# A hybrid encoder layer on one core: two engines instead of one for the first RMS norm of the third and fourth blocks of rows

## The chip, the cores and the metric

The kernel runs on one core of a Trainium2 chip. The core has five engines that each work through a queue of their own in order: TensorE (PE, with its weight loads shown as PEld), VectorE (DVE), ScalarE (ACT), GpSimd (POOL) and SyncE (SP), which here issues nearly all DMAs. The metric is the device time of one execution in microseconds (us), lower is better. The kernel before takes 2622.69 us, the median of 3 runs (2622.18 to 2624.44).

## The reference

One layer of a bidirectional encoder, batch 1, 2048 rows of 1024 features, all float32:

```python
h = rms_norm(x, norm_mix)                      # x: 2048 x 1024
z = h @ w_in                                   # 1024 x 4352
q_a, k_a, v_a, q_b, k_b, v_b, g_a, g_b = split(z)
y_a = windowed_gqa(q_a, k_a, v_a, sink)
y_b = neighborhood_attn(q_b, k_b, v_b, rpb)
gates = sigmoid(concat(g_a, g_b) + b_gate)
x = x + (gates_a * (y_a @ w_proj_a) + gates_b * (y_b @ w_proj_b)) @ w_out
x = x + square(relu(rms_norm(x, norm_mlp) @ w_up)) @ w_down
return rms_norm(x, norm_final)
```

with

```python
def rms_norm(x, g):
    var = mean(x * x, axis=-1)
    return x * rsqrt(var + 1e-6) * g
```

What matters here is the very first norm, `rms_norm(x, norm_mix)`, for rows 1024 to 2047.

## The kernel before

**Blocks and precision.** The 2048 rows are four blocks of 512 rows; a block is four tiles of 128 rows x 1024 features. Every matrix product is made of three matmuls (`mm3`, `mm3s`, lines 200 to 202 and 297 to 299) of operands that are split into a high and a low part: high x high, high x low, low x high. ScalarE makes the high part (a cast, line 293), VectorE the low part (a subtraction, line 294).

**The input projection.** Blocks 0 and 1 go through `w_in` together. A 2 x 2 scheme needs seven products instead of eight; their order is `ORDER = (1, 2, 5, 6, 7, 4, 3)` (line 369). The columns of `w_in` come in nine groups, numbered q = 0 to 8 below (`QUADS`); q = 5 to 8 are the gate columns. For each group a generator `in_quad` runs the seven products. A product has two halves (a = 0, 1) of 12 matmuls of 128x512, each half in a PSUM bank of its own. A bank is used by several products in turn, so between two of them a result must be read out: product 6's bank is read by VectorE (`add(V, u2[a], ps, c1[a])`, line 290) before product 7 writes the same bank, and product 7's before product 4. The operands of a group's seven products come from `in_left`: sums on VectorE (line 290) and splits (lines 293 and 294).

**The third and fourth block.** In column group q = 5 the rows of the third block (b = 2), in q = 6 those of the fourth (b = 3), are prepared beside the products: `x_tiles` loads four tiles (SP, line 362, four DMAs a tile; `xin` has three buffers, the fourth tile lies in the buffer of `in_v2`, tile name `zv2`, shown as `zv`). `normalised(..., by_scalar=True)` then scales every row by the reciprocal root of its mean square: per tile two ScalarE squares with an accumulated sum (line 236), one small VectorE sum of both (line 239), one GpSimd power to -0.5 (line 241), one ScalarE multiplication of the 128x1024 tile by it (line 248). After the third, fourth, fifth and sixth product in program order `turned_out` transposes a quarter of the four tiles each (four VectorE transposes of 128x256, line 260, into a buffer `ze`) and stores it with four DMAs (line 268) to `h1d`, from where later stages load it.

**Shared buffers.** The ring `ze` (`in_e`) has two buffers of 128x1024. Three users share it: the unused outputs of the squares (class `Junk`: `in_e()[:, 0]`), the gate columns that ScalarE copies out of PSUM after product 2 (line 468, stored by line 475), and the four quarters of `turned_out`.

**What sets the order.** The kernel gives priorities by program order; a scheduler places each engine's instructions in a fixed order when the kernel is built. Each engine and SP then run in that order and wait on semaphores. Up to product 7 of q = 5 TensorE's order is the same in both kernels, and from product 2 of q = 7 on the order of every engine is the same again.

Of the kernel before, what the change touches and what calls it, by code (L numbers as in the profile page):

```python
# [8 lines left out]
F32 = mybir.dt.float32  # L9
F32R = mybir.dt.float32r  # L10
AF = mybir.ActivationFunctionType
ALU = mybir.AluOpType
# [3 lines left out]
D = 1024  # L16
# [5 lines left out]
EPS = 1e-6  # L22
P = 128
# [69 lines left out]
def encoder_layer(ctx, tc, x, norm_mix, w_in, b_gate, sink, rpb, w_pa, w_pb, w_out,  # L93
                  norm_mlp, w_up, w_down, norm_final, dist_a, mask_b, out):
    nc = tc.nc
    V, A, G, PE, SY = nc.vector, nc.scalar, nc.gpsimd, nc.tensor, nc.sync

    def pool(name, side=None, space=None, stack=None):
        kw = {"reuse_waits": "tile"} if space is not DRAM else {}
        if side:  # L100
            kw["side"] = side
        if space:
            kw["space"] = space
        return (stack or ctx).enter_context(tc.tile_pool(name=name, bufs=1, **kw))

    def pools(stack, side, tags, name):

        return {t: pool(f"{name}_{t}", side=side, stack=stack) for t in tags}

    cp = pool("cp", side="left")  # L110
# [13 lines left out]
    def T(pl, shape, dt, tag, bufs):  # L124
        n_t[0] += 1
        pl = pl[tag] if isinstance(pl, dict) else pl
        return pl.tile(shape, dt, tag=tag, bufs=bufs, name=f"{tag}_{n_t[0]}")
# [7 lines left out]
    power = cr.tile([P, 1], F32, name="power")  # L135
# [77 lines left out]
    def load_tile(pl, tag, bufs, rows):  # L213
        t = T(pl, [P, D], F32, tag, bufs)
        last_dma[0] = SY.dma_start(t, rows).ins
        return t

    def rstd_shared(pl, t):

        st = T(pl, [P, 4], F32, "st", 4)  # L220
        junk = T(pl, [P, 512], F32, "junk", 1)
        A.activation(junk, t[:, 0:512], AF.Square, accum_out=st[:, 0:1])
        other = T(pl, [P, 512], F32, "junkv", 1)
        V.tensor_tensor_reduce(out=other, in0=t[:, 512:1024], in1=t[:, 512:1024], scale=1.0, scalar=0.0,
                               op0=ALU.mult, op1=ALU.add, accum_out=st[:, 1:2])
        r = st[:, 2 : 3]
        V.scalar_tensor_tensor(out=r, in0=st[:, 0:1], scalar=D * EPS, in1=st[:, 1:2], op0=ALU.add, op1=ALU.add)
        G.tensor_tensor(out=r, in0=r, in1=power, op=ALU.pow)
        return r

    def rstd_of(pl, t, jp=None, mean=False):

        st = T(pl, [P, 4], F32, "st", 4)
        junk = T(pl if jp is None else jp, [P, 512], F32, "junk", 1)
        for n in range(2):
            A.activation(junk, t[:, n * 512 : (n + 1) * 512], AF.Square, scale=float(D) ** -0.5 if mean else 1.0,
                         accum_out=st[:, n : n + 1])
        r = st[:, 2 : 3]
        V.scalar_tensor_tensor(out=r, in0=st[:, 0:1], scalar=EPS if mean else D * EPS, in1=st[:, 1:2],
                               op0=ALU.add, op1=ALU.add)  # L240
        G.tensor_tensor(out=r, in0=r, in1=power, op=ALU.pow)
        return r

    def normalised(pl, tiles, jp=None, by_scalar=False):

        for t in tiles:
            if by_scalar:
                A.activation(t, t, AF.Copy, scale=rstd_of(pl, t, jp, True))
            else:
                V.tensor_scalar(t, t, rstd_of(pl, t, jp), float(D) ** 0.5, ALU.mult, ALU.mult)  # L250

    def turned_out(d, ht, tiles, g, gain=None, queue=None):

        hv = ht.rearrange("p (j t c) -> p t j c", j=8, t=4)
        for t in range(4):
            V.transpose(out=hv[:, t], in_=tiles[t][:, g * 256 : (g + 1) * 256].rearrange("p (j c) -> p j c", j=8))  # L260
        h3 = ht.rearrange("p (j x) -> p j x", j=8)
        if gain is not None:
            (step, n), _ = gain.ap
            gv = bass.AP(gain.tensor, gain.offset + 8 * g, [[step, n], [1, 8], [0, P]])
            V.tensor_tensor(out=h3, in0=h3, in1=gv, op=ALU.mult)
        dv = d.rearrange("(j i) (a x) -> a i j x", i=32, a=4)
        for a in range(4):
            (queue or SY).dma_start(dv[a][:, 8 * g : 8 * g + 8], h3[32 * a : 32 * a + 32])
# [49 lines left out]
    s_z = ExitStack()  # L318
# [14 lines left out]
    xp = pools(s_x, "left", ("xin",), "x0")  # L333
# [20 lines left out]
    def x_tiles(pl, b, bufs):  # L354
        out = []
        for t in range(4):
            xt = T(pl, [P, D], F32, "xin", bufs) if t < bufs else in_v2[0]()
            if b > 1:

                for a in range(4):  # L360
                    r = b * BT + a * P + t * 32
                    SY.dma_start(xt[32 * a : 32 * a + 32], xf[r : r + 32])
            else:
                r = b * BT + t * P
                last_dma[0] = SY.dma_start(xt, xf[r : r + P]).ins
            out.append(xt)
        return out
# [3 lines left out]
    def in_weights(c, w):  # L371

        return [row_half(c, w, p) for p in range(2)]
# [8 lines left out]
    def in_left(ws, w, skip=(), behind=None):  # L382

        a11, a21 = ws[0][:, :, 0:w], ws[0][:, :, w : 2 * w]
        a12, a22 = ws[1][:, :, 0:w], ws[1][:, :, w : 2 * w]

        def parts(src, eng):
            return left_parts(src, w, eng)

        s1, s2 = None, None  # L390
        for n in ORDER:
            if n in skip:
                continue
            with tc.issue_after(behind[0]) if behind else nullcontext():
                if n == 5:
                    s1 = in_sum()[:, :, 0:w]
                    add(V, s1, a21, a22)
                elif n == 6:
                    add(V, a21, a11, a21, ALU.subtract)
                    s2 = in_sum()[:, :, 0:w]  # L400
                    add(V, s2, a22, a21, ALU.subtract)
                elif n == 3:
                    add(V, a12, a12, s2, ALU.subtract)
            yield parts({1: a11, 2: a12, 5: s1, 6: s2, 7: a21, 4: a22, 3: a12}[n], V)
# [137 lines left out]
    for t in tiles[0]:  # L542
        V.tensor_scalar(t, t, rstd_shared(xp, t), float(D) ** 0.5, ALU.mult, ALU.mult)
    right = {n: (in_page[n](), in_page[n]()) for n in (1, 2)}
# [15 lines left out]
    for n, t in enumerate(tiles[1]):  # L560
        V.tensor_scalar(t, t, rstd_shared(xp, t), float(D) ** 0.5, ALU.mult, ALU.mult)
# [10 lines left out]
    for p in range(2):  # L572
        t = T(xp, [P, D], F32, "xin", 8).rearrange("p (k c) -> p k c", k=4)
# [54 lines left out]
    def bias_tables():  # L628
        rp = rpb[0]
        for n, (w, lo_rel) in enumerate(((24, -8), (32, -8), (24, -15))):  # L630
            tb = in_e()[0:BH].rearrange("h a b -> h (a b)")[:, 0 : T_ROWS * w]
            tb3 = tb.rearrange("h (r w) -> h r w", w=w)
            G.memset(tb, 0.0)
            ncol = min(w, 15 - lo_rel + 1)
            first = 15 + lo_rel
            SY.dma_start(tb3[:, T_RO - 7 : T_RO + 8, 0:ncol], rp[:, :, first : first + ncol])

            G.tensor_scalar(tb, tb, 8.0, 1.0, ALU.mult, ALU.mult)
            SY.dma_start(tabs[n], tb)

    for q in range(2, len(QUADS)):
        if q == 5:
            s_v.close()
            in_v2.pop()
            xp = pools(s_z, "right", ("xin", "st"), "x2")
        if q == 7:
            bias_tables()
        lf = list(in_left(ws, 256, (1, 2) if q == 2 else ()))
        if q + 1 < len(QUADS):
            ws = in_weights(*QUADS[q + 1])  # L650
        if q in (5, 6):

            b = q - 3
            xt = x_tiles(xp, b, 3)
            normalised(xp, xt, Junk(), by_scalar=True)
        ops2.extend(lf if q == 2 else ())
        for n, _ in enumerate(quad2 if q == 2 else in_quad(*QUADS[q], iter(lf), right)):
            if q in (5, 6) and 2 <= n < 6:
                turned_out(h1d[b - 2], in_e().rearrange("p k x -> p (k x)"), xt, n - 2)
# [677 lines left out]
    for b in range(NB):  # L1337
# [43 lines left out]
        for t in range(4):  # L1381
            row0 = b * BT + t * P
            xt = load_tile(p4x, "xr", 5, xf[row0 : row0 + P])
# [25 lines left out]
    for m in range(2):  # L1409
        right = next(rights)  # L1410
# [225 lines left out]
```

## Time and profile before

| | value |
|---|---|
| median of 3 runs | 2622.69 us (2622.18 to 2624.44) |
| the profiled execution | 2621.88 us |
| its span | 2620.1 us, so 1.8 us lie around it |
| TensorE busy | 99% of the span |
| VectorE busy | 62% |
| ScalarE busy | 47% |
| GpSimd busy | 14% |
| TensorE idle, 210 to 250 us (third block) | 0.0 us |
| TensorE idle, 250 to 290 us (fourth block) | 3.15 us |

In rows of a timeline the first column is the start in us from the beginning of the span, the second the time (of one instruction, or of several merged ones), then the engine, the line, the operation, the tiles written and read, the shape and the count; in square brackets stands how long the engine was idle before, and what released it. In rows of a table by stretches the columns are, for each engine, busy us and number of instructions, then the granted TensorE clock, the DMA share and GB/s. Line numbers are those of the kernel before.

### The profile page before, as it was taken

The numbers are of one execution on the slowest core, as the hardware profiler recorded it, in microseconds if no ns is written. First come the engines' busy times: TensorE is split into PE (matmuls) and PEld (weight loads), VectorE is DVE, ScalarE is ACT, GpSimd is POOL, SyncE is SP. The second block draws the span as 40 slices with busy tenths as digits, with TensorE's granted clock in tenths as the row PEclk, the third lists the DMA queues.
The fourth block names the chain that finished last, engine by engine and source line by source line (L and its number), as shares of the span: only waits on it lengthen the run. The fifth ranks groups of instructions, "written<-read, shape, count | busy, mean of one in ns | idle before, by whom it ended". The sixth has DMA issues, their size and how long they took to land.

```text
span 2620.1 us, 34509 instructions
## 1 busy us (share of the span) xinstructions
PE 2586.9 (99%) x12140; PEld 2149.8 (82%) x12140; DVE 1625.1 (62%) x2653; ACT 1239.8 (47%) x2261; POOL 358.1 (14%) x431
## 2 busy tenths in 40 slices
PE   8999999999999999999999999999999999999999
PEld 6888788778888888888888888888888888888887
DVE  8765666665544444755567777776656534555766
ACT  5335256666555555633334554644544322322454
POOL 1000114344555541000001000100000000000010
PEclk9999999999999999999999999999999999999999
DMA  5657485455876655954556655854428825445555
GB/s 184 200 156 200 141 243 159 114 155 145 240 219 180 191 144 164 318 177 151 179 178 208 245 205 202 302 191 149 153 101 300 300 101 182 146 146 171 183 194 170
DMA packets 353982, 490.30 MB, mean 187 GB/s; under 512 B 28792, under 2 KB 188664, under 8 KB 351632
## 3 DMA queue, kind: packets, MB, share of 16 engines
q1 hardware_dynamic: 346752, 471.04, 56.8%
q10 hardware_dynamic: 7056, 17.04, 1.8%
q8 instruction: 96, 1.57, 0.2%
q14 instruction: 78, 0.64, 0.1%
HBM read 328.54 MB, written 159.45 MB: 186 GB/s over the span
## 4 chain that ended last, share of the span: by engine, by line
PE 88%; DVE 4%; DMA 4%; ACT 2%; issue 1%; SPq 1%; POOL 0%; DVEq 0%; POOLq 0%; ACTq 0%
PE b L297 15%; PE b L299 15%; PE b L298 15%; PE mm L200 6%; PE mm L202 6%; PE mm L201 6%; PE zb L297 3%; PE zb L299 3%; PE zb L298 2%; PE pt L200 2%; PE pt L201 2%; PE pt L202 2%; PE av L967 2%; PE pt L955 2%; PE s L927 2%
## 5 line engine op out<-in xcount | busy, mean ns | idle before, releaser
L298 PE MATMUL b<-dwh,dah 128*128 128x512 f32 x896 | 348.5, 389 | 0.0
L299 PE MATMUL b<-dwh,dah 128*128 128x512 f32 x896 | 347.6, 389 | 0.0
L297 PE MATMUL b<-dwh,dah 128*128 128x512 f32 x896 | 339.6, 389 | 0.0
L293 ACT CAST dah<-da 128x1024 fp32r<-128x1024 f32 (+1 forms) x128 | 120.9, 945 | 368.6 <-PE b L299 241.8
L294 DVE TENSOR_TENSOR dah<-da,dah 128x1024 fp32r<-128x1024 f32 (+1 forms) x128 | 139.7, 1091 | 224.1 <-ACT dah L293 221.1
L297 PE MATMUL b<-ubh,uwhlb 128*128 128x512 f32 x592 | 230.3, 389 | 0.0
L298 PE MATMUL b<-ubh,uwhlb 128*128 128x512 f32 x592 | 230.3, 389 | 0.0
L299 PE MATMUL b<-ubh,uwhlb 128*128 128x512 f32 x592 | 229.3, 389 | 0.1
L200 PE MATMUL mm<-hT,whl 128*128 128x512 f32 x544 | 218.2, 401 | 0.0
L202 PE MATMUL mm<-hT,whl 128*128 128x512 f32 x544 | 215.1, 395 | 0.0
L201 PE MATMUL mm<-hT,whl 128*128 128x512 f32 x544 | 213.7, 393 | 0.0
L298 PEld LDWEIGHTS b<-dwh,dah 128*128 128x128 f32 x896 | 168.2, 188 | 35.0
L299 PEld LDWEIGHTS b<-dwh,dah 128*128 128x128 f32 x896 | 168.2, 188 | 34.9
L297 PEld LDWEIGHTS b<-dwh,dah 128*128 128x128 f32 x896 | 168.2, 188 | 34.9
L297 PE MATMUL zb<-zh,zwhl 128*128 128x512 f32 x476 | 186.7, 394 | 7.9 <-DVE zc L290 3.4
L298 PE MATMUL zb<-zh,zwhl 128*128 128x512 f32 x476 | 186.4, 392 | 0.0
L299 PE MATMUL zb<-zh,zwhl 128*128 128x512 f32 x476 | 183.7, 392 | 0.3 <-DVE zwhl L294 0.3
L290 DVE TENSOR_TENSOR uc<-b,uc 128x512 f32<-128x512 f32 x160 | 109.2, 689 | 104.2 <-PE b L299 103.2
L1506 POOL TENSOR_TENSOR st<-st,power 128x1 f32<-128x1 f32 x16 | 13.3, 841 | 925.0 <-DVE st L1505 924.9
L297 PEld LDWEIGHTS b<-ubh,uwhlb 128*128 128x128 f32 x592 | 111.1, 188 | 23.8 <-issue 0.4
L299 PEld LDWEIGHTS b<-ubh,uwhlb 128*128 128x128 f32 x592 | 111.1, 188 | 23.5 <-DVE uwhlb L294 0.5
L298 PEld LDWEIGHTS b<-ubh,uwhlb 128*128 128x128 f32 x592 | 111.1, 188 | 23.1
(253 smaller groups left out, 5912.5 us busy)
## 6 DMA issues: line engine op xcount, KB each, us to landing
at<-uc SPq DMA_DIRECT2D x224, 256.0 KB, 2.0
da<-at SPq DMA_DIRECT2D x96, 512.0 KB, 3.7
dw<-in_w_down_dram SPq DMA_DIRECT2D x160, 256.0 KB, 4.8
uraw<-in_w_up_dram SPq DMA_DIRECT2D x32, 1024.0 KB, 6.8
raw<-in_w_in_dram SPq DMA_DIRECT2D x34, 512.0 KB, 4.7
zraw<-in_w_in_dram SPq DMA_DIRECT2D x16, 1024.0 KB, 7.7
z<-zg SPq DMA_DIRECT2D x64, 256.0 KB, 5.1
qa<-qs_a SPq DMA_DIRECT2D x32, 256.0 KB, 8.3
```

Of the source, the lines that this page charges most:

```text
L200: PE.matmul(ps, lh, rh, start=first, stop=False)
L201: PE.matmul(ps, lh, rl, start=False, stop=False)
L202: PE.matmul(ps, ll, rh, start=False, stop=last)
L290: return eng.tensor_tensor(out=out, in0=a, in1=b, op=op).ins
L293: A.copy(hi, src)
L294: return eng.tensor_tensor(out=lo, in0=src, in1=hi.bitcast(F32), op=ALU.subtract).ins
L297: PE.matmul(ps, lh, rh, start=first, stop=False, skip_group_check=True)
L298: PE.matmul(ps, lh, rl, start=False, stop=False, skip_group_check=True)
L299: PE.matmul(ps, ll, rh, start=False, stop=last, skip_group_check=True)
L927: PE.matmul(ps[:, :n], q[:, i, :], kv[:, z, B_R0[i] // 4 : (B_R0[i] + B_NR[i]) // 4, 4 * B_C0[j] : 4 * (B_C0[j] + w)], start=z == 0, stop= ...
L955: PE.transpose(pt[:kp, at + (i - i0) * P : at + (i - i0 + 1) * P], s[i][:, rr : rr + kp], ident)
L967: last = PE.matmul(po[:, i0 * P : (i0 + ni) * P], v[:kp, c, :], src[:kp, o : o + ni * P], start=first, stop=(c == 7 and z == 1), skip_grou ...
```

## The change

For the third and fourth block the tiles 0 and 2 keep their two ScalarE squares. Tiles 1 and 3 get both squares from VectorE: two `tensor_tensor_reduce` of 128x512 with an accumulated sum, whose unused output goes to a tile of its own, `junkv` (one buffer of 128x512), not into the ring `ze`. All four tiles are multiplied by their factor on VectorE (`tensor_scalar`, 128x1024) and none on ScalarE. The constants move with it (the sum instead of the mean of the squares, then a factor 32). The small tiles `st` come from the pool of constants, and `xin` has a pool of three buffers as before.

```diff
+    def rstd_by_vector(pl, t):
+
+        st = T(pl, [P, 4], F32, "st", 4)
+        other = T(pl, [P, 512], F32, "junkv", 1)
+        for n in range(2):
+            half = t[:, n * 512 : (n + 1) * 512]
+            V.tensor_tensor_reduce(out=other, in0=half, in1=half, scale=1.0, scalar=0.0,
+                                   op0=ALU.mult, op1=ALU.add, accum_out=st[:, n : n + 1])
+        r = st[:, 2 : 3]
+        V.scalar_tensor_tensor(out=r, in0=st[:, 0:1], scalar=D * EPS, in1=st[:, 1:2], op0=ALU.add, op1=ALU.add)
+        G.tensor_tensor(out=r, in0=r, in1=power, op=ALU.pow)
+        return r
...
         if q == 5:
             s_v.close()
             in_v2.pop()
-            xp = pools(s_z, "right", ("xin", "st"), "x2")
+            xp = pools(s_z, "right", ("xin", "junkv"), "x2")
+            xp["st"] = cp
...
             b = q - 3
             xt = x_tiles(xp, b, 3)
-            normalised(xp, xt, Junk(), by_scalar=True)
+
+            for n, t in enumerate(xt):
+                r = rstd_by_vector(xp, t) if n % 2 else rstd_of(xp, t, Junk())
+                V.tensor_scalar(t, t, r, float(D) ** 0.5, ALU.mult, ALU.mult)
```

## The prediction

> **What bounds the kernel now.** I read the page first, then the busy time by stretches, then TensorE's waits where the change sits, then each engine's timeline there.
>
> ```profile
> span 2620.1 us, 34509 instructions
> PE 2586.9 (99%) x12140; PEld 2149.8 (82%) x12140; DVE 1625.1 (62%) x2653; ACT 1239.8 (47%) x2261; POOL 358.1 (14%) x431
> ```
> ```profile
> 210.00:250.00 40.00, 40.00 (x180) 33.16 (x179) 25.90 (x42) 18.18 (x32) 2.19 (x4) 1.00 0.80 231
> 250.00:290.00 40.00, 36.85 (x161) 29.61 (x160) 24.73 (x42) 18.48 (x32) 8.38 (x9) 1.00 0.67 197
> ```
> ```profile
> 264.05 0.39 PE L298 MATMUL zb<-zh,zwhl 128*128 128x512 f32 x1
> 264.27 0.39 PE L299 MATMUL zb<-zh,zwhl 128*128 128x512 f32 x1
> 267.58 0.47 PE L297 MATMUL zb<-zh,zwhl 128*128 128x512 f32 x1 [2.92 <-DVE zc L290]
> ...
> 273.38 0.39 PE L297 MATMUL zb<-zh,zwhl 128*128 128x512 f32 x1
> ```
>
> TensorE is busy 99% of the span, so the time is its work plus its idle time. A matmul follows the last one after 0.227 us (264.05 to 264.27). In the third block's stretch (210 to 250) it never idles; in the fourth's (250 to 290) it idles 3.15 us. Of these, 2.92 are one wait at 264.66: product 7 of q = 6 may not write its bank before VectorE has read product 6 out (zc, L290). So at most 3.15 us can be gained here, and whatever delays a VectorE read-out past TensorE's arrival is lost one for one. The last row is product 4's start.
>
> Why was that read-out late? VectorE and ScalarE before it:
>
> ```profile
> 261.37 0.57 ACT L468 COPY ze<-zb 128x512 f32<-128x512 f32 x1
> ...
> 264.30 0.77 DVE L260 STREAM_TRANSPOSE ze<-xin 128x256 f32<-128x256 f32 x2 [2.57 <-DMA zg<-ze]
> 264.99 1.18 DVE L294 TENSOR_TENSOR zwhl<-zraw,zwhl 128x1024 fp32r<-128x1024 f32 x1
> ...
> 266.78 0.65 DVE L290 TENSOR_TENSOR zc<-zb,zc 128x512 f32<-128x512 f32 x1
> ```
>
> ScalarE was behind with squares and scalings, so its gate copy into ze came late, its store freed the buffer late, VectorE idled 2.57 us and then had four transposes and a split ahead of the read-out. The edit aims at this chain.
>
> **The third block, step by step.** Prices:
>
> ```profile
> 3.99 0.69 DVE L224 CUSTOM_DVE_ANT_0 junkv<-xin 128x512 f32<-128x512 f32 x1 [3.99 <-DMA xin<-in_x_dram]
> 4.60 0.08 DVE L224 DVE_READ_ACCUMULATOR2_ANT st<- 128x1 f32 x1
> ...
> 6.08 0.75 DVE L543 TENSOR_SCALAR xin<-xin,st 128x1024 f32<-128x1024 f32 x1
> 6.74 0.15 DVE L227 SCALAR_TENSOR_TENSOR st<-st 128x1 f32<-128x1 f32 x1
> ```
> ```profile
> 219.87 0.63 ACT L236 ACTIVATE ze<-xin 128x512 f32<-128x512 f32 x1
> 220.41 0.19 ACT L236 ACTIVATION_READ_ACCUMULATOR ze<-xin 128x1 f32 x1
> ...
> 223.42 1.14 ACT L248 ACTIVATE xin<-xin,st 128x1024 f32<-128x1024 f32 x1
> ```
>
> Counted from start to start, a VectorE square with its read costs 0.69 (0.61 + 0.08), a factor 0.67 (6.08 to 6.74). A block gives VectorE four squares and four factors, 4 x 0.69 + 4 x 0.67 = 5.4 us. It takes from ScalarE four squares (0.54 to the read, 0.62 with it by the estimate that the read adds 0.08 as on VectorE) and four scalings of 1.14: 7.0 us. ScalarE had room for that, VectorE is what TensorE waits for.
>
> ```profile
> 222.92 1.23 DVE L294 TENSOR_TENSOR zwhl<-zraw,zwhl 128x1024 fp32r<-128x1024 f32 x1 [2.14 <-ACT zwhl L293]
> 224.06 0.15 DVE L239 SCALAR_TENSOR_TENSOR st<-st 128x1 f32<-128x1 f32 x1
> 224.13 0.69 DVE L290 TENSOR_TENSOR zc<-zb,zc 128x512 f32<-128x512 f32 x1
> 226.10 0.69 DVE L290 TENSOR_TENSOR zc<-zb,zc 128x512 f32<-128x512 f32 x1 [1.28 <-PE zb L299]
> ```
> ```profile
> 221.23 0.63 ACT L236 ACTIVATE ze<-xin 128x512 f32<-128x512 f32 x1 [0.64 <-DMA xin<-in_x_dram]
> ```
>
> A split costs 1.14, a sum 0.08, a read-out 0.60 (0.69 until it is done). Product 6's first read-out ended at 224.82; TensorE came to product 7 at 226.05 (its second half ended then: 226.10). Slack 1.2. The changed order puts ahead of this read-out: both squares of tile 1 (which lands at 221.2), a sum, the split, tile 0's factor, a sum, tile 3's first square. That is 221.23 + 0.69 + 0.08 + 0.69 + 1.14 + 0.67 + 0.08 + 0.69 = 225.3, read out by 226.0. The slack is gone; I take 0.2 us of stall (0 to 0.9).
>
> Product 4 needs product 7's read-out (a second kind of zc). Between the two read-outs now stand, from 225.9: sum 0.08, factor 0.67, square 0.69, factor 0.67, product 6's second read-out 0.60, four transposes 4 x 0.34, sum 0.08, split 1.14, two transposes 0.68, and itself 0.69: 6.7 us, done at 232.6. TensorE arrives at 226.05 + 0.2 + 24 x 0.227 = 231.7, so 1.1 us of stall (0.6 to 1.6).
>
> **The fourth block.** A factor waits for GpSimd's power, which now lies on VectorE's path:
>
> ```profile
> 220.93 0.55 POOL L241 TENSOR_TENSOR st<-st,power 128x1 f32<-128x1 f32 x1 [192.49 <-DVE st L239]
> ...
> 255.31 2.00 POOL L241 TENSOR_TENSOR st<-st,power 128x1 f32<-128x1 f32 x2 [26.37 <-DVE st L239]
> ```
> ```profile
> 256.82 1.15 ACT L248 ACTIVATE xin<-xin,st 128x1024 f32<-128x1024 f32 x1 [0.49 <-POOL st L241]
> ```
>
> It takes 0.55 us beside an idle VectorE; the pair of 255.31, beside a 128x1024 VectorE sum, let its first reader go at 256.82, 1.5 us on. So each factor waits 0 to 0.5 us at its place.
>
> The rows of the fourth block load into buffers that the third block's last transposes free:
>
> ```profile
> 239.93 1.10 DVE L260 STREAM_TRANSPOSE ze<-xin 128x256 f32<-128x256 f32 x3 [1.99 <-DMA h1d<-ze]
> ...
> 242.46 0.40 DVE L260 STREAM_TRANSPOSE ze<-zv 128x256 f32<-128x256 f32 x1
> ```
> ```profile
> 233.76 4.92 SPq L268 DMA_DIRECT2D h1d<-ze  x8
> ...
> 253.04 1.76 SPq L362 DMA_DIRECT2D zv<-in_x_dram  x4
> ```
>
> Tile 3's factor now comes after product 7's read-out of the third block, so the first two quarters finish near 236 instead of 235 and their eight stores begin at 235.9, not 233.76. The third quarter waits for a store to land (239.93 before, 242 now), then a read-out (0.60) and a split (1.14) stand ahead of the fourth: transposes end near 246.5 instead of 242.86. SP has four stores and two gate stores ahead of the loads (4 x 0.6 + 0.9) where it had three stores, so the last load leaves near 256.7 instead of 254.8 and tile 1 is there near 256.6.
>
> From there VectorE's order up to product 6's read-out has four squares 2.76, one operand sum 1.14, four small sums 0.32, four factors 2.68, two splits 2.28, eight transposes 2.72, the read-out 0.69: 12.6 us, done at 269.2, with power waits up to 270.5. ScalarE is no longer late there, and the 2.57 us wait for ze goes, but its room is filled by this list. Product 7 starts at 270.0 (269.3 to 270.7) instead of 267.58: +2.4, the third block's stalls contained. Its own stall is then 270.0 - 265.8 = 4.2 us (264.5 + 0.2 + 1.1 = 265.8).
>
> Then product 4:
>
> ```profile
> 271.52 0.68 DVE L290 TENSOR_TENSOR zc<-zb,zc 128x512 f32<-128x512 f32 x1
> 273.60 1.10 DVE L260 STREAM_TRANSPOSE ze<-xin 128x256 f32<-128x256 f32 x3 [1.40 <-DMA h1d<-ze]
> ```
>
> Before, the read-out of product 7 (271.52) stood ahead of the transposes that wait for a store. Now it stands behind them: behind the third quarter (1.36), a split (1.14) and three of the fourth (1.02). The third quarter needs the first one's stores: four issues of 0.6 from 267.9, the last landing 3.8 us after its issue,
>
> ```profile
> h1d<-ze SPq DMA_DIRECT2D x32, 128.0 KB, 3.8
> ```
>
> that is 273.5. So 273.5 + 1.36 + 1.14 + 1.02 + 0.69 + 0.14 (the 267.43 to 267.58 from read-out to matmul) = 277.9 for product 4, where TensorE arrives at 270.0 + 24 x 0.227 = 275.4: a new stall of 2.5 us (0 to 3.3). Against 273.38 before, +4.5 us (2.5 to 6).
>
> **The clock.** An idle TensorE can lose clock:
>
> ```profile
> 52.60 0.47 PE L297 MATMUL zb<-zh,zwhl 128*128 128x512 f32 x1 [1.58 <-DVE zh L521]
> 53.64 0.50 PE L299 MATMUL zb<-zh,zwhl 128*128 128x512 f32 x1 [0.34 <-DVE zwhl L294]
> ...
> 54.87 0.63 PE L297 MATMUL zb<-zh,zwhl 128*128 128x512 f32 x1
> 55.30 0.63 PE L298 MATMUL zb<-zh,zwhl 128*128 128x512 f32 x1
> ```
> ```profile
> 264.30:268.00 3.70, 0.78 (x4) 0.41 (x3) 3.70 (x8) 3.04 (x4) 0.00 (x0) 1.00 0.38 96
> ```
> ```profile
> 55.00:60.00 5.00, 5.00 (x18) 3.96 (x17) 5.00 (x7) 0.00 (x0) 0.00 (x0) 0.72 0.49 117
> ```
>
> After 1.9 us of idling at 51 to 53.6 matmuls came 0.43 us apart (54.87 to 55.30); at a mean clock of 0.72 over 5 us, 1.4 us were lost. After the 2.92 us at 264.66 nothing was: the granted clock stayed 1.00. Two stalls of 4.2 and 2.5 us will likely cost it once; behind the first it lies under the second, behind the second it is paid: 0 to 1.6, I take 0.8. The Trainium skill (TensorE: Matmul & The Clock Gate, "Part 1: The HAM clock gate") says the clock halves after at least one idle window of about 3.4 us, in windows that run freely. By it the 2.5 us stall could cost nothing and the term would be 0, the sum 4.5; the row at 52.60 disagrees, with less than 2 us of idling.
>
> **Sum.** 4.5 + 0.8 = 5.3 us on the profiled 2621.88 gives 2627.2; the median lies 0.8 above that execution, so the forecast is 2628.0 us. From the rest of the kernel I take nothing: every engine's order there is the same.
>
> **The rivals.** 0.2% (about what a measurement of this kernel can tell from no change) is 5.2 us, 2617.4 to 2627.9.
> - *A smaller loss.* If the quarters' stores are issued as early as before, the second stall goes, and 4.5 + 0.8 becomes 1.5 to 3.5: 2624 to 2626. For it: VectorE had idle time there (2.14 and 1.28 us in the rows of 222.92 and 226.10); against it: the fixed order with a read-out behind seven transposes.
> - *A gain.* The edit works: ScalarE's 14 us of work vanish, ze is free early, the read-out of product 6 comes before 264.5. All 3.15 us of idling go: 2619.5. It decides if VectorE's list is done before TensorE arrives, 4.7 us earlier than I add it up.
> - *A larger loss.* Every power beside VectorE takes 1.5 us and the clock halves twice: 1.3 us more at product 7 and 1.6 us of clock: 2630 to 2632. For it the row at 255.31. The Trainium skill (GPSIMD Engine Reference, "8. Key points") says GpSimd contends with VectorE instructions of two SBUF inputs, and the squares are such.
> - *Nothing:* the lost slack is just not used up, 2622.7.
>
> **How the numbers follow.** The forecast (2626 to 2630) 0.40, a smaller loss 0.22, a larger loss 0.24, a gain 0.09, nothing 0.05. The forecast's interval is cut by the 0.2% line; I count 0.26 of its 0.40 as slower, since the clock and the powers push one way. Slower 0.26 + 0.24 = 0.50; faster by over 5.2 us needs more than the stretch's idling, 0.05 for what I don't see; the rest, 0.45, is the same. Leaving out the gain and the far end of the larger loss, the range is 2622.0 to 2632.0; the forecast's own is 2626 to 2630.
>
> **What would show it.** In the changed profile: product 7's wait of q = 6 longer than 2.92 us and still released by VectorE's zc; a second wait of 1 to 3 us at product 4; small waits near 226 and 232; ScalarE's copies near 259 to 261; the fourth quarter's transposes of the third block ending near 246; a clock below 1.00 after 270. I'm wrong if VectorE's zc of product 6 ends before 267, if no second wait comes, or if the difference lies after 300 us.

## The result, and the profile after

| | median us | range | against the kernel before, same chips |
|---|---|---|---|
| before | 2622.42 | 2620.53 to 2628.03 (21 runs) | |
| after | 2626.47 | 2623.75 to 2630.28 (21 runs) | ratio 1.0016, 95% interval 1.0010 to 1.0022 |

The change costs 4.05 us, about 0.15%: less than 0.2%, but the interval of the ratio excludes 1. The forecast of 2628.0 lies 1.5 us above the median.

The profiled execution of the changed kernel took 2623.75 us, the fastest of its 21 runs; 1.8 us lie around its span. First the head of its page, then TensorE's share by stretches (window; its length, then busy us and instructions of PE, PEld, DVE, ACT, POOL; granted clock; DMA share; GB/s):

```profile
span 2621.9 us, 34496 instructions
PE 2586.6 (99%) x12140; PEld 2151.1 (82%) x12140; DVE 1633.6 (62%) x2677; ACT 1227.3 (47%) x2237; POOL 358.9 (14%) x431
```
```profile
210.00:250.00 40.00, 39.03 (x173) 31.80 (x172) 30.00 (x55) 12.21 (x20) 3.45 (x4) 1.00 0.78 224
...
260.00:270.00 10.00, 5.29 (x22) 4.08 (x21) 8.92 (x20) 2.23 (x3) 1.40 (x1) 0.93 0.53 171
270.00:280.00 10.00, 10.00 (x41) 8.12 (x40) 8.08 (x15) 1.06 (x1) 0.00 (x0) 0.90 0.79 220
```

The change did what it says: ScalarE's busy time fell by 12.5 us, VectorE's grew by 8.5. TensorE now idles 0.97 us in the third block's stretch and 4.71 in the fourth's. From the second wait on the granted clock is below 1.00, over 20 us by 0.07 x 10 + 0.10 x 10 = 1.7 us. TensorE's timeline shows both waits:

```profile
231.29 0.47 PE L310 MATMUL zb<-zh,zwhl 128*128 128x512 f32 x1 [0.97 <-DVE zc L303]
...
268.91 0.76 PE L310 MATMUL zb<-zh,zwhl 128*128 128x512 f32 x1 [4.71 <-DVE zc L303]
269.47 0.63 PE L311 MATMUL zb<-zh,zwhl 128*128 128x512 f32 x1
269.90 0.63 PE L312 MATMUL zb<-zh,zwhl 128*128 128x512 f32 x1
...
275.93 0.39 PE L310 MATMUL zb<-zh,zwhl 128*128 128x512 f32 x1
```

231.29 is product 4 of q = 5, 268.91 product 7 of q = 6, 275.93 its product 4. (Line numbers of the changed kernel are 13 higher here: L310 is the old L297, L303 the old L290, L273 the old L260.) From 269.47 on matmuls come 0.43 us apart instead of 0.227. At product 4 of q = 6 no wait is shown. VectorE ahead of these read-outs:

```profile
261.93 1.09 DVE L273 STREAM_TRANSPOSE ze<-xin 128x256 f32<-128x256 f32 x3
...
264.64 0.75 DVE L672 TENSOR_SCALAR zv<-zv,st 128x1024 f32<-128x1024 f32 x1 [0.44 <-POOL st L241]
265.31 1.22 DVE L307 TENSOR_TENSOR zwhl<-zraw,zwhl 128x1024 fp32r<-128x1024 f32 x1
266.44 0.44 DVE L273 STREAM_TRANSPOSE ze<-zv 128x256 f32<-128x256 f32 x1
266.81 1.05 DVE L273 STREAM_TRANSPOSE ze<-xin 128x256 f32<-128x256 f32 x3
267.79 0.40 DVE L273 STREAM_TRANSPOSE ze<-zv 128x256 f32<-128x256 f32 x1
268.11 1.25 DVE L303 TENSOR_TENSOR zc<-zb,zc 128x512 f32<-128x512 f32 x2
271.36 1.10 DVE L273 STREAM_TRANSPOSE ze<-xin 128x256 f32<-128x256 f32 x3 [2.00 <-DMA h1d<-ze]
...
274.82 0.65 DVE L303 TENSOR_TENSOR zc<-zb,zc 128x512 f32<-128x512 f32 x1
```

Product 6's read-out (268.11) stands behind both first quarters' eight transposes and two splits; VectorE is 89% busy from 260 to 270.

**Two yardsticks.** Two executions of one kernel differ by several us elsewhere, so the stretch is measured by itself: from ScalarE's first copy of product 1 of q = 5 to the first matmul of the stage after (first of L200). Before and after:

```profile
206.10 0.59 ACT L498 COPY zc<-zb 128x512 f32<-128x512 f32 x1 [1.47 <-PE zb L299]
```
```profile
361.80 0.40 PE L200 MATMUL mm<-hT,whl 128*128 128x512 f32 x1
```
```profile
204.79 0.59 ACT L511 COPY zc<-zb 128x512 f32<-128x512 f32 x1 [1.47 <-PE zb L312]
```
```profile
365.16 0.40 PE L200 MATMUL mm<-hT,whl 128*128 128x512 f32 x1
```

That is 155.7 us before, 160.4 after: +4.7. (206.10 is the first of product 1's two copies, though the expectation of `e5_layout` below calls it the second.) The second yardstick is when product 6's first read-out of q = 6 starts, from the same copy: 266.78 - 206.10 = 60.7 before, 268.11 - 204.79 = 63.3 after. Times of two profiles are compared from this copy on, never as they stand, since the changed profile reaches it 1.31 us earlier. Both yardsticks are in the table for every run below, with the clock that was lost (in us, worked out as above from the windows of 10 us between 250 and 290).

| run | median minus before, us (ratio, 95% interval) | wait at product 4, q = 5 | wait at product 7, q = 6 | read-out after the copy | clock | stretch |
|---|---|---|---|---|---|---|
| before | | 0 | 2.92 | 60.7 | 0 | 155.7 |
| e5_layout (old work) | -0.6 (0.9991 to 1.0009) | 0 | 3.01 | 61.0 | 1.7 | 158.1 |
| after | +4.05 (1.0010 to 1.0022) | 0.97 | 4.71 | 63.3 | 1.7 | 160.4 |
| e6_after_again | +3.1 (1.0003 to 1.0021) | 0.67 | 5.57 | 63.8 | 3.5 | 162.1 |
| e1_third | +0.7 (0.9994 to 1.0011) | 0.68 | 2.98 | 61.4 | 0 | 157.0 |
| e2_fourth | 0.0 (0.9992 to 1.0010) | 0 | 2.04 | 63.0 | 3.4 | 160.0 |
| e3_squares | +2.8 (1.0003 to 1.0021) | 1.21 | 3.88 | 62.6 | 3.4 | 161.2 |
| e4_factors | +0.9 (0.9993 to 1.0011) | 1.58 | 1.96 | 62.2 | 1.7 | 159.7 |
| e7_before_shift | -3.5 (0.9980 to 0.9998) | 0 | 1.27 | 59.7 | 0 | 154.6 |
| e8_after_shift | -0.4 (0.9991 to 1.0009) | 0.64 | 2.65 | 61.0 | 0 | 156.1 |
| e9_warm | +5.4 (1.0010 to 1.0028) | 0.68 | 1.89 | 63.9 | 0 | 161.0 |
| e10_all_squares | +2.8 (1.0001 to 1.0018) | 0.56 | 3.78 | 62.5 | 1.7 | 159.4 |
| e11_one_tile | -1.7 (0.9982 to 1.0000) | 0 | 2.24 | 60.1 | 1.7 | 156.4 |
| e12_raw_rows | +2.7 (1.0001 to 1.0019) | 0.84 | 3.33 | 61.9 | 1.7 | 160.7 |

The medians are of 11 runs (after: 21) beside 15 to 33 of the kernel before. An interval spans about 4.7 us (after: about 3), so single differences of 1 or 2 us are told by the columns of the profile, not by the medians. Some of the lost clock fell into the wait itself, where no matmul ran and nothing was paid: 0.1 us in the changed profile, 0.5 to 0.6 in `e3_squares` and `e6_after_again`. The table leaves out three kinds of waits: for ScalarE's copy of product 1, near 255 (1.84 us in `e2_fourth`, 0.88 in `e4_factors` and `e7_before_shift`, at most 0.41 elsewhere); one of 0.38 us at product 7 of q = 5 in `e10_all_squares`; and 1.34 us at product 4 of q = 6 in `e12_raw_rows` and 1.94 in `e9_warm`, shown below. All waits in its two columns are released by VectorE's zc, but for the 1.21 us of `e3_squares`, which ScalarE's cast ends.

### The profile page after: what moved, and what is told of

Its sections match the earlier page's. It is cut to its first block, busy times and chain, and to the rows that moved or that the text cites. A ratio compares the mean times of both kernels' runs of the same rounds, so it can differ in the third digit from the quotient of the medians.

```text
span 2621.9 us, 34496 instructions
## 1 busy us (share of the span) xinstructions
PE 2586.6 (99%) x12140; PEld 2151.1 (82%) x12140; DVE 1633.6 (62%) x2677; ACT 1227.3 (47%) x2237; POOL 358.9 (14%) x431
## 3 DMA queue, kind: packets, MB, share of 16 engines
q1 hardware_dynamic: 346752, 471.04, 57.4%
## 4 chain that ended last, share of the span: by engine, by line
PE 92%; DVE 3%; DMA 2%; ACT 1%; issue 1%; SPq 1%; POOL 0%; POOLq 0%; DVEq 0%; ACTq 0%
PE b L310 15%; PE b L311 15%; PE b L312 15%; PE mm L200 6%; PE mm L202 6%; PE mm L201 6%; PE zb L310 3%; PE zb L312 3%; PE zb L311 3%; PE pt L200 2%; PE pt L201 2%; PE pt L202 2%; PE av L984 2%; PE pt L972 2%; PE s L944 2%; PE pt L801 1%
## 5 line engine op out<-in xcount | busy, mean ns | idle before, releaser
L310 PE MATMUL b<-dwh,dah 128*128 128x512 f32 x896 | 339.6, 389 | 0.0
L310 PE MATMUL b<-ubh,uwhlb 128*128 128x512 f32 x592 | 230.2, 389 | 0.0
L200 PE MATMUL mm<-hT,whl 128*128 128x512 f32 x544 | 218.1, 401 | 0.0
L310 PE MATMUL zb<-zh,zwhl 128*128 128x512 f32 x476 | 187.1, 395 | 10.9 <-DVE zc L303 6.9
L310 PEld LDWEIGHTS b<-dwh,dah 128*128 128x128 f32 x896 | 168.2, 188 | 35.0
L303 DVE TENSOR_TENSOR uc<-b,uc 128x512 f32<-128x512 f32 x160 | 109.1, 688 | 104.4 <-PE b L312 103.3
L310 PEld LDWEIGHTS b<-ubh,uwhlb 128*128 128x128 f32 x592 | 111.1, 188 | 23.4 <-issue 0.4
```

Of the source, the lines that this page charges most:

```text
L200: PE.matmul(ps, lh, rh, start=first, stop=False)
L303: return eng.tensor_tensor(out=out, in0=a, in1=b, op=op).ins
L310: PE.matmul(ps, lh, rh, start=first, stop=False, skip_group_check=True)
```

## The experiments

The theory at the start: VectorE's added 5.4 us a block push its read-outs past TensorE's arrival, and the longer wait costs clock.

**One block at a time.**

```diff
-            for n, t in enumerate(xt):
-                r = rstd_by_vector(xp, t) if n % 2 else rstd_of(xp, t, Junk())
-                V.tensor_scalar(t, t, r, float(D) ** 0.5, ALU.mult, ALU.mult)
+            if b == 2:      # e1_third; b == 3 in e2_fourth
+                for n, t in enumerate(xt):
+                    r = rstd_by_vector(xp, t) if n % 2 else rstd_of(xp, t, Junk())
+                    V.tensor_scalar(t, t, r, float(D) ** 0.5, ALU.mult, ALU.mult)
+            else:
+                normalised(xp, xt, Junk(), by_scalar=True)
```

> The third block as changed, the fourth block's rows all by ScalarE as before, the tiles in memory placed as in the changed kernel. Theory (VectorE's added 5.4 us a block put its read-outs behind TensorE's arrival): one stall of about 1.0 us at product 4 of q = 5, as in the changed kernel, the 2.9 us wait of q = 6 as before or up to 0.8 longer because the loads come later: +1.0 us on before (0.5 to 2.0). Rival A (the new place of the tiles in memory or the run, not the work): +4 us. Rival B (the third block's delay is what makes the fourth late): +3 or more, with the wait of q = 6 above 4 us.

> The fourth block as changed, the third block's rows all by ScalarE as before. Theory: no stall near 231, the wait at product 7 of q = 6 is 4.5 to 5.3 us (TensorE arrives 1 us earlier, the loads at most 1 us earlier), then half clock for 2 to 4 us: +3 us on before (2.3 to 3.8). Rival A (place in memory): +4. Rival B (the fourth block is late only because the third block's delay moves its loads): +1 or less, the wait of q = 6 near 3 us and the clock whole.

The third block alone gave 0.68 us at product 4 of q = 5, a wait of 2.98 us in q = 6 as before, and a stretch 1.3 us longer: as the theory has it, and rival B falls. The fourth block alone put the read-out 2.3 us later than before. Its wait at product 7 was only 2.04 us, since TensorE came late: in the same column group it had already waited 1.84 us, up to 254.70, for a ScalarE copy, and the clock was lowered twice (3.4 us), once ahead of product 7. Without the clock its stretch is 156.6. The median shows no loss, the forecast said +3: a miss that the theory did not explain. By the median rival B would stand here; by the read-out, which is late without any work of the third block, it falls. The two parts (+0.7 and 0.0) do not add up to the whole (+4.05 and +3.1).

**Squares alone, factors alone.**

```diff
...
+                r = rstd_by_vector(xp, t, True) if n % 2 else rstd_of(xp, t, Junk(), True)
+                A.activation(t, t, AF.Copy, scale=r)                                        # e3_squares
...
```
```diff
...
+                V.tensor_scalar(t, t, rstd_of(xp, t, Junk()), float(D) ** 0.5, ALU.mult, ALU.mult)  # e4_factors
...
```

> Both blocks; VectorE makes every other tile's squares as in the changed kernel, but all factors are ScalarE's again. VectorE has 2.8 us a block more than before, ScalarE 2.5 us less. Theory: the losses go with VectorE's list, so about half: no stall near 231, the wait of q = 6 3 to 4 us, no half clock or a short one: +1 us on before (0 to 2). Rival A (place in memory): +4. Rival C (only what ScalarE gives up matters, VectorE has room): -1 to 0.

> Both blocks; VectorE makes all factors as in the changed kernel, but all squares are ScalarE's, with the squares going to a ze buffer as before. VectorE has 2.7 us a block more than before and waits for GpSimd's power ahead of each factor, ScalarE 4.6 us less. Theory: +1.5 us on before (0.5 to 2.5), the wait of q = 6 3.5 to 4.5 us. Rival A (place in memory): +4. Rival C (ScalarE's backlog of 14 us is the limit, VectorE has room): -1 to -3, the wait of q = 6 under 2 us. Rival D (it is the wait for the power, not the work, that makes VectorE late): nearly all of the loss, +3 to +4, with this kernel and none without factors on VectorE.

Either half of the work gives more than half of the read-out's delay: 62.6 and 62.2 against 63.3 with both and 60.7 with none. So the delay does not go with the amount alone. Three forecasts were missed: the squares cost 2.8 us instead of 0 to 2 and show a wait of 1.21 us in q = 5 instead of none, and the wait at product 7 with the factors was 1.96 us instead of 3.5 to 4.5. Rival C falls, as neither kernel gains, and rival D, as the squares without factors lose more than the factors. In both kernels the second quarter's transposes, ahead of the read-out, wait for a `ze` buffer that a gate column's store frees, first `e3_squares` (where the first quarter had waited 2.16 us for ScalarE's last factor), then `e4_factors`:

```profile
266.18 1.10 DVE L273 STREAM_TRANSPOSE ze<-xin 128x256 f32<-128x256 f32 x3 [0.79 <-DMA zg<-ze]
```
```profile
265.70 1.10 DVE L273 STREAM_TRANSPOSE ze<-xin 128x256 f32<-128x256 f32 x3 [0.85 <-DMA zg<-ze]
```

**The place in memory, and the clock from run to run.** `e5_layout` has the old instructions with the new place of the `st` tiles; `e6_after_again` is the changed kernel.

```diff
+            if q == 5:
+                T(xp, [P, 512], F32, "junkv", 1)
+            normalised(xp, xt, Junk(), by_scalar=True)
```

> Every instruction of the kernel before, in the same order, with the small st tiles of the two blocks in the place that they have in the changed kernel. It tells what the place alone does, and gives a second profile of the old work. From the second copy of q = 5's product 1 by ScalarE to the first matmul of the stage after (the first of L200) the kernel before took 361.80 - 206.10 = 155.7 us, the changed one 365.16 - 204.79 = 160.4. Theory (the work on VectorE does it): 155.7 (155.2 to 156.5), one wait of 2.9 us at product 7 of q = 6, a clock of 1.00, median as before. Rival A (the place of the tiles): 158 or more.

> The changed kernel once more, for a second profile: the first one showed the fastest of its runs, 2.7 us under their median. Theory: the same two waits (1.0 us at product 4 of q = 5, 4.7 at product 7 of q = 6), the same 160.4 us from copy to first L200 within 0.5, and the 2.7 us come from other places or from the clock. If the stretch itself varies: a second wait at product 4 of q = 6, or half clock for another 3 us, 162 or more.

The place does nothing: -0.6 us, and the read-out where it was. But the second profile of the old work differs from the first in the clock. The matmul and the windows of the old work in `e5_layout`:

```profile
267.27 0.47 PE L310 MATMUL zb<-zh,zwhl 128*128 128x512 f32 x1 [3.01 <-DVE zc L303]
```
```profile
260.00:270.00 10.00, 6.99 (x27) 5.38 (x26) 6.34 (x14) 7.03 (x11) 1.10 (x2) 0.89 0.40 128
270.00:280.00 10.00, 10.00 (x43) 8.18 (x42) 8.31 (x16) 1.06 (x1) 0.00 (x0) 0.94 1.05 320
```

After a wait of 3.01 us 0.11 x 10 + 0.06 x 10 = 1.7 us of clock were lost; in the profile before, 2.92 us cost nothing. The second profile of the changed kernel, its wait and the window behind it:

```profile
270.15 0.76 PE L310 MATMUL zb<-zh,zwhl 128*128 128x512 f32 x1 [5.57 <-DVE zc L303]
```
```profile
270.00:280.00 10.00, 9.85 (x32) 7.92 (x33) 6.50 (x15) 1.06 (x1) 0.00 (x0) 0.70 0.78 213
```

3.0 us were lost there alone, and the stretch reaches 162.1, as the second reading of its expectation had it. The two pairs give +4.7 and +4.0 us for the stretch, about what the medians give (+4.05, +3.1).

**The order of VectorE's list.** In q = 6 the quarters' transposes are put one product later and behind the read-out at hand, in the kernel before and in the changed one:

```diff
...
-                    add(V, u2[a], ps, c1[a])
+                    last_read[0] = add(V, u2[a], ps, c1[a])
...
-            if q in (5, 6) and 2 <= n < 6:
-                turned_out(h1d[b - 2], in_e().rearrange("p k x -> p (k x)"), xt, n - 2)
+            if q in (5, 6) and q - 3 <= n < q + 1:
+                with tc.issue_after(last_read[0]) if q == 6 else nullcontext():
+                    turned_out(h1d[b - 2], in_e().rearrange("p k x -> p (k x)"), xt, n - q + 3)
```

> The kernel before, where only the order of VectorE's list in q = 6 is other: the transposes of the fourth block's quarters come one product later and behind the read-out of the product at hand. Theory (a read-out that stands behind other work of VectorE is what TensorE waits for): product 6's first read-out is no longer behind four transposes and can follow the split near 265; the wait of 2.9 us falls to 0.5 to 1: -2 us on before (-3 to -1). Rival E (ScalarE's backlog holds the read-out, not VectorE's order): 0. Rival F (the later transposes, stores and loads come back as a wait in the next stage): 0 or +1, with a new wait after 275.

> The changed kernel with the same other order in q = 6. Theory: eight transposes (2.7 us) no longer stand ahead of product 6's read-out; the wait of 4.7 us becomes about 2, the clock stays whole, the wait of 1.0 us at product 4 of q = 5 remains: 157 to 158 us from copy to first L200, +0.5 to +1.5 us on before, 3 less than the changed kernel. Rival G (it is the squares, sums and factors that are late because the rows' loads are, whatever the order): the wait stays at 4 us or more. Rival F: the wait moves to product 4 or to the end of the block.

VectorE and TensorE of `e7_before_shift`:

```profile
263.94 1.23 DVE L294 TENSOR_TENSOR zwhl<-zraw,zwhl 128x1024 fp32r<-128x1024 f32 x1 [2.24 <-ACT zwhl L293]
265.08 0.68 DVE L290 TENSOR_TENSOR zc<-zb,zc 128x512 f32<-128x512 f32 x1
```
```profile
265.91 0.47 PE L297 MATMUL zb<-zh,zwhl 128*128 128x512 f32 x1 [1.27 <-DVE zc L290]
```

The read-out comes at 265.08, one split behind ScalarE's cast; the wait fell from 2.92 to 1.27 and the median by 3.5 us (ratio 0.9989, 0.9980 to 0.9998). Its stretch is 1.1 and 3.6 us shorter than those of the two profiles of the old work, without and with a lowered clock. The gain is larger than the 1 to 3 us expected; one profile each does not tell how much of it is clock. This kernel beats both others. The same order in the changed kernel, where eight transposes stood ahead instead of four, moved the read-out from 63.3 to 61.0 and the wait to 2.65; it takes 3.5 us off the changed kernel's difference. Rivals E, F and G fall: no new wait of note follows in the block.

So the order is worth 3.5 us in either kernel, and by that it does not explain what the change costs: with the transposes out of the way the changed kernel is still 3.1 us behind the old work (medians of 2621.79 and 2618.69, runs side by side, whose ranges overlap by 0.4 us), and its read-out comes at 61.0 instead of 59.7. Ahead of that read-out stand then the squares, factors and splits, without a wait for `ze`. In `e8_after_shift`:

```profile
266.05 1.28 DVE L303 TENSOR_TENSOR zc<-zb,zc 128x512 f32<-128x512 f32 x2
```
```profile
266.87 0.47 PE L310 MATMUL zb<-zh,zwhl 128*128 128x512 f32 x1 [2.65 <-DVE zc L303]
```

**The clock, and the wait that it hides.** Sixteen unused matmuls between products 6 and 7 of q = 6:

```diff
...
+            if n == 7 and extra:      # extra = 16 in q = 6
+                unused = zbank(tpool, 2)
+                with tc.issue_after(last_mm):
+                    for _ in range(extra):
+                        last_mm = PE.matmul(unused, hl[:, 0, 0, 0:P], rh[:, 0], start=True, stop=True,
+                                            skip_group_check=True).ins
...
```

> The changed kernel with 16 more matmuls (their product is not used) between products 6 and 7 of q = 6, where TensorE waits 4.7 to 5.6 us: 16 x 0.227 = 3.6 us, so 1.1 to 2.0 us of the wait are left idle; the order of everything else is kept. Theory (the half clock after that wait comes from idling, and it hides a wait at product 4 that VectorE's order sets): product 7 starts no later, the clock stays 1.00 from 260 to 280, and a wait of about 1.2 us for zc appears at product 4 of q = 6; from copy to first L200 159 to 161 us (against 160.4 and 162.1), 0 to 2 us faster than the changed kernel. Rival H (the clock is lowered for another reason than idling): clock below 0.95 after 268 as before, no gain. Rival I (no wait would be left at product 4): 2 to 3 us faster than the changed kernel, no new wait.

TensorE and its windows in `e9_warm`:

```profile
263.95 3.79 PE L500 MATMUL zb<-zh,zwhl 128*128 128x512 f32 x16
...
269.63 0.47 PE L310 MATMUL zb<-zh,zwhl 128*128 128x512 f32 x1 [1.89 <-DVE zc L303]
...
277.30 0.47 PE L310 MATMUL zb<-zh,zwhl 128*128 128x512 f32 x1 [1.94 <-DVE zc L303]
```
```profile
260.00:270.00 10.00, 8.11 (x37) 6.43 (x36) 9.49 (x20) 3.10 (x4) 2.74 (x3) 1.00 0.52 172
270.00:280.00 10.00, 8.06 (x36) 6.35 (x35) 7.42 (x15) 1.04 (x1) 0.69 (x2) 1.00 0.81 193
```

With most of the wait filled the clock stays at 1.00, and a wait of 1.94 us appears at product 4. VectorE's order behind the read-out is a little other here (two quarters stand ahead of a split), so 1.94 us is not the size of the wait in the changed kernel. An estimate from that kernel's own rows is 1.2 us: at full clock TensorE would be at product 4 at 268.91 + 24 x 0.227 = 274.4, and VectorE's read-out ends at 274.82 + 0.65 = 275.5, to which the 0.14 us from read-out to matmul is added. The half clock of the changed kernel lay over it. Rivals H and I fall. Nothing is gained, as the stretch of 161.0 shows. The median is even 1 to 2 us above the changed kernel's, within the intervals.

**More work on VectorE, less of it, and none.**

```diff
...
+                r = rstd_by_vector(xp, t)                                                   # e10_all_squares
...
```
```diff
...
+                r = rstd_by_vector(xp, t, True) if q == 6 and n == 1 else rstd_of(xp, t, Junk(), True)
+                A.activation(t, t, AF.Copy, scale=r)                 # e11_one_tile, with the order of e7_before_shift
...
```
```diff
...
+            if q == 5:                                                                      # e12_raw_rows
+                for n, t in enumerate(xt):
...
```

> The changed kernel with the squares of all four tiles of both blocks on VectorE, none on ScalarE: 2.8 us more of VectorE a block. Theory (VectorE's list sets the waits): the wait at product 4 of q = 5 grows from 1.0 to 2 to 4 us, the one at product 7 of q = 6 stays at 5 to 7; +7 us on before (5.5 to 10). Rival C (ScalarE's share is what is late): the waits shrink, +2 or less. Rival J (the two losses are the rows' loads and the power waits, and the squares are hidden among them): as the changed kernel, +4.

> The kernel before with the other order of VectorE's list in q = 6 (as in the run before_shift), and of the change only the squares of tile 1 of the fourth block on VectorE (1.4 us, where it idled 4.35 us from 256.6 to 260.9); all factors and the rest stay ScalarE's. Theory: ScalarE gives up 1.6 us ahead of its casts, the split that stands ahead of product 6's read-out can start 1 to 1.2 us earlier, the wait of 1.3 us at product 7 falls to 0 to 0.4: -1 us on before_shift, -4 to -5 on before. Rival K (ScalarE's casts wait for something else): as before_shift, -3.5. Rival C': any work added to VectorE's list delays the read-out: -2.

> The changed kernel without squares, sums, powers and factors of the fourth block: its rows are transposed as they were loaded, so the last outputs are not the reference's. Loads, transposes, splits, read-outs and their order (eight transposes and two splits ahead of product 6's read-out in q = 6) stay. It tells whether the chain of squares, power and factor that starts when the last tile lands (259.4 in the changed kernel) is what makes the read-out late, or the order and the loads alone. Theory (the last tile's chain, 259.4 to 265.3, which the transposes behind it and the read-out behind these must wait out): transposes and splits done by 263.5, the wait at product 7 is 0 to 0.8 instead of 4.7, the clock whole; the 0.7 to 1.0 us at product 4 of q = 5 remain: 153.5 to 155 us from copy to first L200, -1 to -3 us on before. Rival L (loads and order alone): the wait is 2 us or more, 157 us or more.

All three went against the theory. With 2.8 us a block more on VectorE (`e10_all_squares`) the read-out came earlier than in the changed kernel (62.5) and the wait in q = 6 shrank to 3.78 us, which lies between rivals C and J. There the last two tiles are so late that their transposes fell behind the read-out: four instead of eight stand ahead, 4 x 0.34 = 1.4 us less. So this run does not show that more work costs nothing. With none of the fourth block's norm work (`e12_raw_rows`) the wait was still 3.33 us. VectorE in that run, SP's queue, and a wait at product 4:

```profile
261.67 1.10 DVE L273 STREAM_TRANSPOSE ze<-xin 128x256 f32<-128x256 f32 x3 [8.93 <-DMA zg<-ze]
262.69 0.40 DVE L273 STREAM_TRANSPOSE ze<-zv 128x256 f32<-128x256 f32 x1
263.02 2.31 DVE L307 TENSOR_TENSOR zwhl<-zraw,zwhl 128x1024 fp32r<-128x1024 f32 x2
266.14 1.10 DVE L273 STREAM_TRANSPOSE ze<-xin 128x256 f32<-128x256 f32 x3 [0.81 <-DMA zg<-ze]
267.17 0.41 DVE L273 STREAM_TRANSPOSE ze<-zv 128x256 f32<-128x256 f32 x1
267.49 0.65 DVE L303 TENSOR_TENSOR zc<-zb,zc 128x512 f32<-128x512 f32 x1
```
```profile
248.54 5.40 SPq L375 DMA_DIRECT2D xin<-in_x_dram  x11
254.25 1.90 SPq L375 DMA_DIRECT2D zv<-in_x_dram  x4
256.54 0.35 SPq L488 DMA_DIRECT2D zg<-ze  x1
263.13 0.33 SPq L281 DMA_DIRECT2D h1d<-ze  x1
263.55 0.40 SPq L488 DMA_DIRECT2D zg<-ze  x1
```
```profile
276.93 0.47 PE L310 MATMUL zb<-zh,zwhl 128*128 128x512 f32 x1 [1.34 <-DVE zc L303]
```

VectorE idles 8.93 us: the first quarter may not be written before a gate column's store has freed its `ze` buffer. That store is issued at 256.54, behind the 15 row loads on SP, and frees the buffer at 261.67. The second gate store stands behind the first quarter's own (263.13), so the second quarter waits until 266.14. The read-out behind them starts at 267.49 although VectorE had idled. Rival L holds for this kernel. It does not hold word for word for the changed one, whose SP queue has another order:

```profile
258.21 2.39 SPq L488 DMA_DIRECT2D zg<-ze  x2
...
266.91 4.46 SPq L281 DMA_DIRECT2D h1d<-ze  x8
```

There both gate stores leave together, ahead of any store of a quarter, and VectorE waits for no `ze` buffer before the read-out; its waits from 260 on are 0.44 us for GpSimd. In `e3_squares` and `e4_factors` the second gate store stands behind a quarter's store as here.

In `e11_one_tile` ScalarE's order changed as well:

```profile
261.17 1.16 ACT L674 ACTIVATE xin<-xin,st 128x1024 f32<-128x1024 f32 x1
262.23 0.62 ACT L249 ACTIVATE ze<-zv 128x512 f32<-128x512 f32 x1
...
262.84 1.14 ACT L674 ACTIVATE xin<-xin,st 128x1024 f32<-128x1024 f32 x1
263.88 1.03 ACT L306 CAST zwhl<-zraw 128x1024 fp32r<-128x1024 f32 x1
```
```profile
266.93 0.64 PE L310 MATMUL zb<-zh,zwhl 128*128 128x512 f32 x1 [2.24 <-DVE zc L303]
```

A square and a second scaling (262.84) now stand between the first scaling and the cast, which starts at 263.88; counted from the copy that is 57.9, against 262.87 - 205.43 = 57.4 in `e7_before_shift`. The cast came later, not earlier, and the gain of 1 us did not come. Rival K is right, in that the cast waits for ScalarE's order.

## Why the prediction came out as it did

The direction, the place and the releaser were right, the time within the range; the sum was 1.3 us too large (5.3 against 4.05), and one reason behind it was only half of the story.

- *Third block, product 7, +0.2:* there was no wait. VectorE's read-out ran from 223.74 and TensorE came to product 7 at 224.58, just in time.
- *Third block, product 4, 1.1 (0.6 to 1.6):* 0.97 and 0.67 in the two profiles of the changed kernel. Right, though its own terms give 232.6 - 231.7 = 0.9, or 1.0 with the 0.14 us from read-out to matmul.
- *Fourth block, product 7 starts 2.4 us later, its own wait 4.2:* the read-out is 2.6 and 2.8 us later by the second yardstick (against the profile before and `e5_layout`), the wait 4.71 and 5.57. The start is right, the wait in the second profile 1.4 us longer than said.
- *The reason given for it, VectorE's list of 12.6 us, is right for this kernel, but not the only chain.* VectorE's list did end late, with waits of at most 0.44 us in it from 255 us on, and it is what leaves the changed kernel 3.1 us behind when the transposes are out of the way. But the prediction took each added us as a us of delay, and it is not: leaving the whole norm of the fourth block out brings the read-out only 1.4 us forward (63.3 to 61.9). A second chain ends shortly before the first: loads on SP, a gate column's store, a free `ze` buffer, the eight transposes. With half of the work or none the last wait ahead of the read-out is the one for this ring, and the read-out comes at 62.6, 62.2 and 61.9. "The 2.57 us wait for ze goes" was true of this kernel and no more: VectorE's list had grown over that wait, and without the list it is back (8.93 and 0.81 us).
- *Second stall at product 4, 2.5 (0 to 3.3):* none is shown, and the prediction had named that as a sign of being wrong. About 1.2 us of it lie under the half clock, by the estimate above. The step was mis-sized by the landing of the stores: the third quarter's transposes were put 3.5 us behind product 7's start (273.5 against 270.0) and began 2.45 behind it (271.36 against 268.91). From product 7 to product 4 it took 275.93 - 268.91 = 7.0 us instead of 277.9 - 270.0 = 7.9, half clock included.
- *Clock, 0.8 (0 to 1.6):* this is the term of the sum that fails. The half clock came behind the first wait, and lay over the second, where the prediction had put its price at nothing; it should not have been added. At product 4 the changed kernel is 3.9 us late with the clock in it (275.93 - 204.79 = 71.1 us from the copy, 273.38 - 206.10 = 67.3 before), where the prediction had 4.5 without it. The pair of `e6_after_again` and `e5_layout` gives 3.8 (278.37 - 205.60 and 274.45 - 205.52), though 2.9 us of clock were paid behind its wait: the old work, taken as free of it, lost 1.7 there.
- *The rivals:* the gain did not come: ScalarE's 12.5 us went, but VectorE's list was not done when TensorE arrived. The smaller loss asked for stores as early as before; they left 266.91 - 204.79 = 62.1 us from the copy, against 266.88 - 206.10 = 60.8 before and 61.8 predicted, so its condition did not come, and yet the second stall stayed hidden. The larger loss asked for 1.5 us at every power; in the fourth block of the changed profile they took 0.55 to 1.40, and VectorE waited 0.43 and 0.44 us for two of them.
- *Placed after 300 us:* a wait of 1.20 us near 353 in the changed profile, 0.23 in the one before, was not predicted. The old work has it too in `e5_layout` (1.17), so it is no effect of the change that these runs can show.

What stays open: why the fourth block alone shows no loss in its median, while its one profile has a stretch of 160.0. The clock explains 3.4 us of that in this execution; how often the others paid it was not seen. Nor do the runs show how much of the read-out's delay in the changed kernel the `ze` ring alone would leave, as the runs without part of the work also change SP's order, and why four transposes stand ahead in the old work and eight here: the scheduler fixes that order.

## What to carry to other kernels

When an engine waits for a read-out, look at what stands ahead of that read-out in the reader's queue and what each of those instructions waits for, before moving work between engines: here moving the norm from ScalarE to VectorE made the read-out up to 3 us later, and taking the transposes from in front of it (four in the old work, eight in the changed kernel) gave 3.5 us in either without moving any work. An engine that is emptied in front of a full buffer ring gains little (`e12_raw_rows`). Before a wait is priced, ask what else would fill the same time: here a half clock and a later wait lay over each other, and their sum was not paid.

## What the hardware showed that was not expected

The clock was lost in portions: 1.7 us in `e5_layout`, the first changed profile, `e4_factors`, `e10_all_squares`, `e11_one_tile` and `e12_raw_rows`, 3.4 or 3.5 in `e2_fourth`, `e3_squares` and `e6_after_again`, nothing in between. In `e5_layout` matmuls came 0.43 us apart for 3.3 us (268.16 to 271.45). Between 1.8 and 3.0 us the length of a wait does not tell whether it costs a portion: waits of 1.84 and 2.04 us (`e2_fourth`), 1.96 (`e4_factors`) and 2.24 (`e11_one_tile`) were followed by one, 1.89 and 1.94 (`e9_warm`), 2.65 (`e8_after_shift`), 2.92 (before) and 2.98 (`e1_third`) were not, 3.01 (`e5_layout`) was; all from 3.33 up were. The Trainium skill (TensorE: Matmul & The Clock Gate, "Part 1: The HAM clock gate") says that the clock halves after at least one idle window of about 3.4 us, in windows that run freely. By an estimate from the Trainium skill's window, 3.4 us at half clock lose 1.7 us, and the portion agrees. That a whole idle window is needed does not, by the four waits of 1.84 to 2.24 us.
